# A two-layer trunk (attention with short convolution, gated linear attention, gated MLPs): GLA's state and read products are issued in one piece, the MLP's value weights are loaded before the gate's, and two small steps get a scheduling priority

## The chip, the cores and the metric

The kernel runs on one core of a Trainium2 chip. The core has a matrix engine (PE, TensorE), a vector engine (DVE, VectorE), a scalar engine (ACT, ScalarE), GpSimd (POOL) and a queue that issues DMAs (SP, SyncE). PE reads from SBUF and writes into PSUM, which has eight banks of 128 partitions by 512 float32 numbers; DVE and ACT read PSUM and SBUF and write SBUF. The metric is device time in microseconds (us) of one launch; the median over three runs of the kernel before is 1228.61 us (1227.54 to 1229.41).

## The reference

512 tokens, width 1024, two layers, all in float32. Cut to what matters here:

```python
def _sliding_window_sink_attention(q, k, v, sinks):      # layer 0, in blocks of 128 queries
    ...
    probs = jax.nn.softmax(jnp.concatenate([scores, sink], axis=-1), axis=-1)[..., :-1]
    out = jnp.einsum('bnhgqk,bnkhd->bnqhgd', probs.astype(v.dtype), vband)

def _gla_chunked(q, k, v, log_a):                        # layer 1: 4 heads, keys 128, values 256
    def step(state, inp):
        ...
        scores = jnp.einsum('bhtd,bhsd,bhtsd->bhts', qi, ki, decay)
        o_intra = jnp.einsum('bhts,bhsv->bhtv', scores, vi)
        state = jnp.exp(g_end)[..., None] * state + jnp.einsum(
            'bhsd,bhsv->bhdv', ki * jnp.exp(g_end[:, :, None, :] - gi), vi)
        return state, o_inter + o_intra                  # o_inter = (q * exp(g)) @ state

def _conv_ffn(h, w_up, conv_w, conv_b, w_down):          # each layer; w_up is 1024 x 5632
    u = _causal_depthwise_conv(h @ w_up, conv_w) + conv_b
    gate, up = jnp.split(u, 2, axis=-1)
    return (jax.nn.gelu(gate, approximate=False) * up) @ w_down
```

Each layer is a mixer (attention with a short convolution in layer 0, gated linear attention, GLA, in layer 1), then this MLP, then a per-layer embedding with a sigmoid gate.

## The kernel before

**Precision.** A float32 product is made of three fast passes. An operand is split into a high part (ACT copies it into the type fp32r) and a low part (DVE subtracts: source minus high part). `mm3` then issues high by high, high by low and low by high: L157, L158 and L159 for plain products, L848, L849 and L850 for the blocks of the seven-product scheme below. `cut` splits a piece of weights (high at L137, low at L138); `cut_blocks` does the same for blocks (high at L796, low at L797). Weights come by DMA on SP's queue into two buffers of 1 MB, `raw`; split parts live in three buffers each, `wh` and `wl`. Products go to PSUM banks of two rings of four, `ps` and `pa`. Small products (attention scores, GLA) run in full float32 with one instruction each in the code; the trace holds two records of each.

**Scheduling.** Except where an order is set by hand, a scheduler orders the instructions of each engine from the order in the program and from when their operands would be ready; `tc.high_priority(offset=n)` moves the instructions inside it up, as if they stood n earlier in the program. Semaphores between the engines follow from the tiles. A PSUM bank is tracked as a whole: a product into one half of a bank waits for a reader of the other half that stands earlier in the program.

**Attention (layer 0).** For each of four blocks of queries, `scores` (products L584) gives probabilities, `probs` transposes them (L631) and copies the transposed ones from PSUM to `pT`: ACT's copy at L638, and for the second half of the window DVE's at L636. The first block has only ACT's copies, two of them. `conv_taps` around it computes the short convolution; L682, L684 and L686 are its steps.

**Up-projection (`ffn`).** The 2816 columns of gate and of value are worked on in eleven groups of 256. For the gate's 256 columns, a block scheme with seven products in place of eight is used (`seven_forms`, `seven`): the piece `rg` is split as it is (`plain`), then DVE forms differences of blocks in place (L820, L821, L828, L830), which are split too: `t13`, `t2` (half as large, formed at L828 in `more_forms` and split at once in the program) and `last`. The value's 256 columns take plain products, in two halves: column block `w1` opens a group, `w0` comes in its middle. So each group has six splits, in the program's order w1, plain, t13, t2, w0, last. `loaded(d)` issues the two loads of group d, gate first, value second. The first of the two takes the buffer of the previous group's value piece, which is free after the low part of `w0`; the second takes that of the gate piece, free after the low part of `last`. PE's order in this stage is written by hand (`manual_schedule`): group d+1 opens with three quarters of the `w1` product, then steps of `seven` and parts of the value products alternate. ACT and DVE are ordered by the scheduler. Inside `seven`, ACT copies PSUM blocks from one bank to another between two products that add to them (L859, L860, L869, L873; L866 puts one aside). After a group, `taps` does the width-3 convolution (DVE L899, L902, L905, L908, ACT L906), ACT the Gelu (L1036), DVE the product of gate and value (L948 or L958).

**GLA (layer 1).** The list of calls at the end of the mixer sets the program's order; the scheduler fits the small products between projections. For head h, `base` forms cumulative decays and the product of even keys and queries (L1614); `diag` sums it over the partitions by a product with ones (L1620) and writes the diagonal of the score matrix `sc` (L1621, DVE); `decay` makes the decayed keys and queries of one level (DVE L1634 to L1642, ACT L1637); `level` multiplies them (L1655, for the coarsest level L1658) and writes them into `sc` (L1666, L1668); `level_pairs` does the two finest levels (L1693, L1699, L1704). `state` makes three products of decayed keys and values (L1750), two to a bank, and folds each into the running state `st` (first by ACT's copy L1757, then DVE's L1752). `read` makes for each of four chunks scores by values (L1773) and, but for the first, queries by state (L1775), two chunks to a bank, then squares and sums (ACT L1777). `turn` transposes (L1789) after a scaling by DVE (L1782).

Of the kernel before, what the change touches and what calls it, by code (L numbers as in the profile page):

```python
# [18 lines left out]
P = 128  # L19
# [37 lines left out]
class Kernel:  # L57
# [366 lines left out]
    def mixer0(self):  # L424
        nc, a, tc = self.nc, self.a, self.tc
        with tc.tile_pool(name="m0", bufs=1) as mp:
# [190 lines left out]
            def probs(t):  # L617

                s, den = ss[t], dens[t]
                w = 2 * P if t else P  # L620
                nc.vector.tensor_tensor(
                    s[:, 4:, :w], s[:, 4:, :w], den[:, 4:].unsqueeze(2).to_broadcast([P, 4, w]), ALU.mult
                )
                for head in range(4):
                    nc.scalar.activation(s[:, head, :w], s[:, head, :w], AF.Copy, scale=den[:, head : head + 1])
                pT = pTs[t] = mp.tile([P, 2, NQ, P], F32, tag="pT", name=self.nm("pT"), bufs=1)
                for g in range(2):
                    for c in range(2 if t else 1):
                        pb = self.pa()
                        for hh in range(4):  # L630
                            nc.tensor.transpose(  # L631
                                pb[:, hh * P : (hh + 1) * P], s[:, 4 * g + hh, c * P : (c + 1) * P], self.ident
                            )
                        o = pT[:, c, 4 * g : 4 * g + 4, :].rearrange("p a b -> p (a b)")
                        if c:
                            nc.vector.tensor_copy(o, pb)  # L636
                        else:
                            nc.scalar.copy(o, pb)  # L638

            def mix(t):  # L640

# [182 lines left out]
    def more_forms(self, ev, od):  # L824

        nc = self.nc
        b11, b21, b22 = ev[:, :, :P], od[:, :, :P], od[:, :, P:]
        nc.vector.tensor_tensor(b11, b22, b11, ALU.subtract)  # L828
        t2 = self.cut_blocks(b11, False)
        nc.vector.tensor_tensor(b21, b21, b11, ALU.subtract)  # L830
        return t2

# [46 lines left out]
    def ffn(self, i, project, next_gain):  # L879
# [8 lines left out]
        with tc.tile_pool(name=f"ffn{i}", bufs=1) as fp:  # L888
# [22 lines left out]
                    )  # L911

            def loaded(d):
                out = [self.raw(ND, 256) for _ in range(2)]
                for raw, c0 in zip(out, (256 * d, DFF + 256 * d)):
                    nc.sync.dma_start(raw, wu[:, :, c0 : c0 + 256])
                return out

# [6 lines left out]

            def prepare(d):

                rg, rv = loaded(d)
                w1 = column(rv, 1)
                ev, od = self.by_parity(rg)  # L930
                ws = self.seven_forms(ev, od, rg)
                return self.seven(od, ws, xg, self.forms), w1, column(rv, 0)
# [542 lines left out]
    def mixer1(self):  # L1475
# [4 lines left out]
        with tc.tile_pool(name="m1", bufs=1) as mp:  # L1480
# [261 lines left out]
            def state(h):  # L1742

                kt, tot = Fs[h, "kt"], Fs[h, "off"][2]
                st = mp.tile([P, NT - 1, GDV], F32, tag="st", name=self.nm("st"), bufs=1)
                for i in range(NT - 1):
                    if i % 2 == 0:
                        pp = self.pa()
                    u = pp[:, (i % 2) * GDV : (i % 2 + 1) * GDV]
                    mm(u, kt[:, i * P : (i + 1) * P], vt[i][:, h * GDV : (h + 1) * GDV], start=True, stop=True)  # L1750
                    if i:
                        nc.vector.scalar_tensor_tensor(  # L1752
                            out=st[:, i, :], in0=st[:, i - 1, :], scalar=tot[:, i, :], in1=u,
                            op0=ALU.mult, op1=ALU.add,
                        )
                    else:
                        nc.scalar.copy(st[:, i, :], u)  # L1757
                Fs[h, "st"] = st
# [3 lines left out]
            def read(h):  # L1762

                sc = scores[h]
                Ec, st = Fs[h, "off"][1], Fs[h, "st"]
                oss = self.few(NT, "ss")
                pos = []
                for j in range(NT):
                    if j % 2 == 0:
                        pp = self.pa()  # L1770
                    po = pp[:, (j % 2) * GDV : (j % 2 + 1) * GDV]
                    c = slice(j * P, (j + 1) * P)
                    mm(po, sc[:, c], vt[j][:, h * GDV : (h + 1) * GDV], start=True, stop=j == 0)  # L1773
                    if j:
                        mm(po, Ec[:, c], st[:, j - 1, :], start=False, stop=True)  # L1775
                    sq = self.sp.tile([P, GDV], F32, tag="sq", name=self.nm("osq"), bufs=2)
                    nc.scalar.activation(sq, po, AF.Square, accum_out=oss[:, j : j + 1])  # L1777
                    pos.append(po)
                rh = self.few(NT, "rq")
                self.rsqrt(rh, oss, 1.0 / GDV)  # L1780
                for j in range(NT):
                    nc.vector.tensor_scalar_mul(sc[:, j * GDV : (j + 1) * GDV], pos[j], rh[:, j : j + 1])  # L1782
# [33 lines left out]
            key(w, 1)  # L1816
            w = pair_w(256)
            base(0)
            decay(0, lo)
            query(w, 2)  # L1820
            diag(0)
            level(0, lo)
            decay(0, hi)
            decay_off(0)
# [114 lines left out]
```

## Time and profile before

| | us |
|---|---|
| median of three runs | 1228.61 (1227.54 to 1229.41) |
| the profiled execution's own time | 1228.92 |
| its span | 1227.1 |
| PE busy | 1217.1 |
| DVE busy | 970.1 |
| ACT busy | 665.0 |
| a 1 MB load of up-projection weights, from issue to landing (median of 44) | 5.0 |

The span is the time from the first to the last instruction of the profiled execution; its own time also holds what lies around the span. A row of a timeline gives the start from the span's start, the duration (for several instructions in a row, from the first's start to the last's end), the engine, the line of the kernel, the operation, the tile written and those read, the shape, the count, and in brackets how long the engine had been idle before it and what released it. Matmuls are pipelined: each is listed with a duration longer than the step from one to the next.

### The profile page before, as it was taken

What the parts mean: (1) busy time and instruction counts of PE and PEld (TensorE: products, weight loads), DVE (VectorE), ACT (ScalarE), POOL (GpSimd) and SP (SyncE); (2) the same over time, 40 slices, a digit from 0 to 9 for tenths busy, and PEclk for the clock granted to TensorE, in tenths of its full rate; (3) what the DMA queues carried; (4) which work ended last, traced back from release to release, by engine and by line L of the source; (5) the groups of instructions that cost most, each with busy time, mean ns of one, the idle gap of its engine ahead of it and who ended that gap; (6) DMA issues with size and microseconds to landing.
All of it is one profiled execution on the core that took longest, in us unless ns stands there. A gap on an engine that the chain in (4) does not pass through costs nothing.

```text
span 1227.1 us, 17714 instructions
## 1 busy us (share of the span) xinstructions
PE 1217.1 (99%) x7028; PEld 1053.4 (86%) x7028; DVE 970.1 (79%) x1537; ACT 665.0 (54%) x1084; POOL 44.2 (4%) x64
## 2 busy tenths in 40 slices
PE   9999999999999999999999999999999999999998
PEld 8877789989999889888978978889998989889887
DVE  6886587899998986746679875777999889987595
ACT  7466455556555644534563644555555545645374
POOL 3500000000000000000100000000000000000000
PEclk9999999999999999999999999999999999999999
DMA  7221322423232332222332212323242422422601
GB/s 217 92 82 51 90 69 69 138 69 127 80 109 98 100 124 95 95 93 87 113 91 69 85 53 69 103 66 107 69 138 69 138 69 96 144 96 95 205 1 69
DMA packets 111128, 117.61 MB, mean 96 GB/s; under 512 B 2841, under 2 KB 106323, under 8 KB 111045
## 3 DMA queue, kind: packets, MB, share of 16 engines
q1 hardware_dynamic: 109680, 115.35, 28.9%
q8 instruction: 55, 0.90, 0.3%
q0 software_dynamic: 560, 0.42, 0.3%
q10 hardware_dynamic: 804, 0.70, 0.2%
q14 instruction: 29, 0.23, 0.1%
HBM read 114.37 MB, written 2.10 MB: 95 GB/s over the span
## 4 chain that ended last, share of the span: by engine, by line
PE 83%; DVE 10%; ACT 2%; issue 2%; DMA 2%; POOL 1%; DVEq 0%; ACTq 0%; POOLq 0%
PE ps L157 13%; PE ps L158 12%; PE ps L159 12%; PE pa L158 6%; PE pa L157 6%; PE pa L159 6%; PE ps L850 5%; PE ps L848 5%; PE ps L849 5%; PE pa L850 2%; PE pa L849 2%; PE pa L848 2%; DMA raw<-in_ffn_w_up_dram 2%; DVE wl L138 1%; DVE wl L797 1%
## 5 line engine op out<-in xcount | busy, mean ns | idle before, releaser
L137 ACT ACTIVATE wh<-raw 128x1024 fp32r<-128x1024 f32 (+4 forms) x154 | 152.2, 991 | 162.2 <-PE ps L158 112.8
L138 DVE TENSOR_TENSOR wl<-raw,wh 128x1024 fp32r<-128x1024 f32 (+4 forms) x154 | 175.2, 1139 | 50.5 <-ACT wh L137 48.9
L796 ACT ACTIVATE wh<-raw 128x1024 fp32r<-128x1024 f32 x78 | 82.4, 1056 | 113.7 <-DVE raw L821 66.6
L908 DVE SCALAR_TENSOR_TENSOR zt<-z,vfa,zt 128x510 f32<-128x510 f32 (+1 forms) x176 | 131.4, 747 | 9.6 <-ACT zt L906 8.8
L797 DVE TENSOR_TENSOR wl<-raw,wh 128x1024 fp32r<-128x1024 f32 x78 | 95.4, 1223 | 14.5 <-ACT wh L796 14.4
L906 ACT ACTIVATE zt<-z,vfb 128x512 f32<-128x512 f32 x88 | 70.6, 808 | 17.0 <-DVE four L958 5.4
L157 PE MATMUL ps<-b,wh 128*128 128x512 f32 x192 | 76.8, 400 | 0.0
L159 PE MATMUL ps<-b,wl 128*128 128x512 f32 x192 | 75.7, 394 | 0.0
L158 PE MATMUL ps<-b,wh 128*128 128x512 f32 x192 | 75.4, 393 | 0.0
L159 PE MATMUL pa<-b,wl 128*128 128x512 f32 x176 | 68.7, 390 | 0.4 <-DVE wl L138 0.4
L157 PE MATMUL pa<-b,wh 128*128 128x512 f32 x176 | 69.0, 392 | 0.0
L157 PE MATMUL pa<-a,wh 128*128 128x512 f32 x176 | 69.0, 392 | 0.0
L158 PE MATMUL pa<-b,wh 128*128 128x512 f32 x176 | 69.0, 392 | 0.0
L158 PE MATMUL pa<-a,wh 128*128 128x512 f32 x176 | 69.0, 392 | 0.0
L159 PE MATMUL pa<-a,wl 128*128 128x512 f32 x176 | 68.6, 390 | 0.0
L850 PE MATMUL ps<-four,wl 128*128 128x256 f32 x232 | 65.7, 283 | 0.0
L849 PE MATMUL ps<-four,wh 128*128 128x256 f32 x232 | 65.6, 283 | 0.0
L848 PE MATMUL ps<-four,wh 128*128 128x256 f32 x232 | 65.6, 283 | 0.0
L157 PE MATMUL ps<-a,wh 128*128 128x512 f32 x160 | 63.1, 394 | 0.0
L158 PE MATMUL ps<-a,wh 128*128 128x512 f32 x160 | 62.5, 391 | 0.0
L159 PE MATMUL ps<-a,wl 128*128 128x512 f32 x160 | 62.4, 390 | 0.0
L157 PE MATMUL ps<-uh,wh 128*128 128x512 f32 x128 | 50.3, 393 | 0.0
(470 smaller groups left out, 3526.8 us busy)
## 6 DMA issues: line engine op xcount, KB each, us to landing
raw<-in_ffn_w_up_dram SPq DMA_DIRECT2D x44, 1024.0 KB, 5.0
raw<-in_ffn_w_down_dram SPq DMA_DIRECT2D x13, 1024.0 KB, 4.8
raw<-in_hy_w_in_dram SPq DMA_DIRECT2D x8, 1024.0 KB, 5.0
raw<-in_gla_w_in_dram SPq DMA_DIRECT2D x8, 1024.0 KB, 5.1
raw<-in_ffn_w_down_dram SPq DMA_DIRECT2D x8, 768.0 KB, 4.2
raw<-in_ple_w_gate_dram SPq DMA_DIRECT2D x6, 1024.0 KB, 4.8
raw<-in_hy_w_out_dram SPq DMA_DIRECT2D x16, 256.0 KB, 3.9
raw<-in_gla_w_out_dram SPq DMA_DIRECT2D x4, 1024.0 KB, 4.7
```

What stands on the lines that cost most here:

```text
L137: nc.scalar.activation(hv, v, AF.Copy)
L138: nc.vector.tensor_tensor(lv, v, hv.bitcast(F32), ALU.subtract)
L157: mm(out, lh, rh, start=start, stop=False, **kw)
L158: mm(out, lh, rl, start=False, stop=False, **kw)
L159: mm(out, ll, rh, start=False, stop=stop, **kw)
L796: nc.scalar.activation(h, src, AF.Copy)
L797: nc.vector.tensor_tensor(l, src, h.bitcast(F32), ALU.subtract)
L848: mm(out, wh, xh, start=first and j == 0, stop=False, **kw)
L849: mm(out, wh, xl, start=False, stop=False, **kw)
L850: mm(out, wl, xh, start=False, stop=j == ND // 2 - 1, **kw)
L906: nc.scalar.activation(y, z, AF.Identity, scale=w2[:, f : f + 1], bias=bb[:, f : f + 1])
L908: nc.vector.scalar_tensor_tensor(out=y[:, tap:], in0=z[:, : S - tap], scalar=w[:, f : f + 1], in1=y[:, tap:], op0=ALU.mult, op1=ALU.add,)
```

## The change

Six edits in the program's text:

- `probs`: the copies of the first block's probabilities get a priority of 100 positions; those of the other blocks one of 0.
- `more_forms`: the split of `t2`, high and low part, gets a priority of 40.
- `loaded` and `prepare`: the value's piece is allocated and loaded first, the gate's second. The splits stay in the same order.
- `state`: all three products are issued first, then the three steps that read them.
- `read`: all products of the four chunks are issued first, then the four squares.
- the list of calls: `diag(0)` stands ahead of `decay(0, lo)` and `query(w, 2)` instead of behind them.

```diff
                         o = pT[:, c, 4 * g : 4 * g + 4, :].rearrange("p a b -> p (a b)")
-                        if c:
-                            nc.vector.tensor_copy(o, pb)
-                        else:
-                            nc.scalar.copy(o, pb)
+                        with tc.high_priority(offset=0 if t else 100):
+                            if c:
+                                nc.vector.tensor_copy(o, pb)
+                            else:
+                                nc.scalar.copy(o, pb)
...
         nc.vector.tensor_tensor(b11, b22, b11, ALU.subtract)
-        t2 = self.cut_blocks(b11, False)
+        with self.tc.high_priority(offset=40):
+            t2 = self.cut_blocks(b11, False)
         nc.vector.tensor_tensor(b21, b21, b11, ALU.subtract)
...
                 out = [self.raw(ND, 256) for _ in range(2)]
-                for raw, c0 in zip(out, (256 * d, DFF + 256 * d)):
+                for raw, c0 in zip(out, (DFF + 256 * d, 256 * d)):
                     nc.sync.dma_start(raw, wu[:, :, c0 : c0 + 256])
...
-                rg, rv = loaded(d)
+                rv, rg = loaded(d)
...
+                us = []
                 for i in range(NT - 1):
                     if i % 2 == 0:
                         pp = self.pa()
-                    u = pp[:, (i % 2) * GDV : (i % 2 + 1) * GDV]
-                    mm(u, kt[:, i * P : (i + 1) * P], vt[i][:, h * GDV : (h + 1) * GDV], start=True, stop=True)
+                    us.append(pp[:, (i % 2) * GDV : (i % 2 + 1) * GDV])
+                    mm(us[i], kt[:, i * P : (i + 1) * P], vt[i][:, h * GDV : (h + 1) * GDV], start=True, stop=True)
+                for i, u in enumerate(us):
                     if i:
...
                         mm(po, Ec[:, c], st[:, j - 1, :], start=False, stop=True)
+                    pos.append(po)
+                for j, po in enumerate(pos):
                     sq = self.sp.tile([P, GDV], F32, tag="sq", name=self.nm("osq"), bufs=2)
                     nc.scalar.activation(sq, po, AF.Square, accum_out=oss[:, j : j + 1])
-                    pos.append(po)
...
             base(0)
+            diag(0)
             decay(0, lo)
             query(w, 2)
-            diag(0)
             level(0, lo)
```

In the order of instructions that results on each engine, PE's order changes in GLA alone: `diag(0)`'s product stands 24 matmuls earlier, and the products of `state` and `read` stand together where a projection matmul stood between them before. In the up-projection the orders of ACT and DVE change, and on SP which of a group's two pieces is loaded first. No instruction is added or removed.

## The prediction

> **What bounds the kernel now.** I read the page's head first, then the table of windows over three stages, then PE's own waits, then the timelines around each wait.
>
> ```profile
> PE 1217.1 (99%) x7028; PEld 1053.4 (86%) x7028; DVE 970.1 (79%) x1537; ACT 665.0 (54%) x1084; POOL 44.2 (4%) x64
> ```
>
> TensorE (PE) is busy for 99% of the span. So nothing that only shortens VectorE (DVE) or ScalarE (ACT) pays; what pays is PE time lost to a late operand. The change adds and removes no product, so it can win only such lost time. The windows cover the two up-projections (from the first value product of the first group to that of the tenth) and one crowded piece of GLA; the columns are the stretch's length, then busy time of PE, weight load, DVE, ACT, POOL, the granted clock and the DMA share.
>
> ```profile
> 205.12:395.83 190.71, 190.20 (x1191) 171.73 (x1189) 172.72 (x231) 109.06 (x155) 0.00 (x0) 1.00 0.30 100
> 837.21:1028.45 191.24, 190.35 (x1191) 171.76 (x1190) 171.28 (x230) 108.18 (x154) 0.00 (x0) 1.00 0.30 100
> 640.00:660.00 20.00, 18.85 (x126) 15.27 (x124) 19.62 (x47) 7.18 (x14) 0.00 (x0) 1.00 0.12 36
> ```
>
> The granted clock is 1.00 throughout, so time is counted in products and stalls alone. PE's waits (line that waited, what released it, total, times, longest):
>
> ```profile
> PE pa L1655 <- DVE sc L1621: 1.1, 1, 1.1
> PE ps L850 <- DVE t L797: 1.0, 2, 0.5
> PE pa L584 <- ACT pT L638: 1.0, 1, 1.0
> PE pa L159 <- DVE wl L138: 0.4, 1, 0.4
> PE pa L158 <- DVE wl L138: 0.2, 1, 0.2
> PE pa L1658 <- DVE sc L1621: 0.2, 1, 0.2
> ```
>
> These six lines sum to 3.9 us, and they are all in places that the change touches. The list understates: ends of matmuls are modelled, so the loss is better read from start to start. In the up-projection the first window starts with its first group; the next group starts at 226.16, so that one that runs without a visible wait takes 226.16 - 205.12 = 21.04 us:
>
> ```profile
> 226.16 0.40 PE L157 MATMUL pa<-a,wh 128*128 128x512 f32 x1
> ```
>
> Nine such groups are 189.36 us. The two windows above last 190.71 and 191.24, so 1.35 and 1.88 us are lost in them, 3.2 together, where the waits list shows only 1.6. The Trainium skill ("Perfetto Trace Analysis", the note that opens the page) calls matmul busy time a bad metric because matmuls are pipelined; the 3.2 against 1.6 agrees. A sum made from the waits list alone would be 1228.9 - 3.9 = 1225.0.
>
> **Up-projection: values loaded first, t2's split ahead.** Each group needs two 1 MB pieces, gate and value. Today the gate's goes out first, when the value's last split has freed a buffer, and the value's second, when the gate's last split has. But the next group starts with a value product. The activity on the raw pieces around the second group, and ACT and DVE there:
>
> ```profile
> L916 SPq DMA_DIRECT2D raw<-in_ffn_w_up_dram x2: 368/368/368, 214.7 to 217.8; - x2
> ```
> ```profile
> 223.97 1.06 ACT L137 ACTIVATE wh<-raw 128x1024 fp32r<-128x1024 f32 x1 [1.62 <-DMA raw<-in_ffn_w_up_dram]
> ```
> ```profile
> 225.06 1.23 DVE L138 TENSOR_TENSOR wl<-raw,wh 128x1024 fp32r<-128x1024 f32 x1 [0.89 <-ACT wh L137]
> ```
>
> The gate goes out at 214.7, the value at 217.8; it lands 6.2 us later, ACT makes the high part (1.06), DVE the low part, done at 226.29, while the group starts at 226.16. That is a loop load, split, load with no reserve, and its jitter is the 0.4 and 0.2 of L159 and L158 and the smaller slips that only the windows show. After the change the value takes the issue at 214.7: landing 220.9, high part 222.0, low part by 223.2, 3 us before its use. The gate goes out at 217.8 and lands at 224.0; its first low part is done by 224.0 + 1.06 + 1.23 = 226.3, and PE reaches the first gate product after three quarters of the value product, eighteen matmuls of 0.23 (723.57 to 723.80 in the last fence of this part): 4.2 us into the group, at 230.4. Reserve 4 us. Both places in SyncE's (SP's) queue stay taken by the same size, in exchanged order; no other load is passed. As w1's split no longer ends the loop, the group's splits all move up, until PE itself is what frees their buffers.
>
> t2's low part (0.69 us on DVE) stands, in the changed order, straight behind L830, the form after t2's own; today w0's 1.23 us split slips in between:
>
> ```profile
> 255.61 0.69 DVE L830 TENSOR_TENSOR raw<-raw 128x512 f32<-128x512 f32 x1
> 256.21 1.23 DVE L138 TENSOR_TENSOR wl<-raw,wh 128x1024 fp32r<-128x1024 f32 x1
> 257.34 0.69 DVE L797 TENSOR_TENSOR t<-raw,t 128x512 fp32r<-128x512 f32 x1
> ```
> ```profile
> 257.31 0.28 PE L849 MATMUL ps<-four,t 128*128 128x256 f32 x1
> 258.09 0.39 PE L850 MATMUL ps<-four,t 128*128 128x256 f32 x1 [0.50 <-DVE t L797]
> ```
>
> PE steps from L849 to L850 in 0.78 instead of 0.12, a loss of 0.66; with t2 first its low part would run from 256.21 to 256.9, before L850's 257.43; its high part is there, since PE's first two products of t2 had begun. w0's split then ends 0.6 later, near 258.0, and its low part is used after the ten steps of 0.12 that t2's twelve still have, and two of 0.23: 257.43 + 1.2 + 0.46 = 259.1. The second such stall (the waits list counts two) goes the same way. I take 3.0 of the 3.2 us. Bounds: 1.4 (the t2 stalls and the L159 one, 0.5 + 0.5 + 0.4 by the waits list) and 3.2.
>
> **Copies of the probabilities (first block).** ACT copies two halves; the second has to wait behind a convolution step that itself waits for DVE:
>
> ```profile
> 72.19 0.57 ACT L638 COPY pT<-pa 128x512 f32<-128x512 f32 x1
> 73.25 0.72 ACT L684 ACTIVATE cy<-pad,vec 128x512 f32<-128x512 f32 x1 [0.48 <-DVE pad L682]
> 73.88 0.57 ACT L638 COPY pT<-pa 128x512 f32<-128x512 f32 x1
> ```
>
> With the priority the second copy stands straight behind the first: start 72.66 instead of 73.88, 1.22 us sooner. PE's L584 waited for exactly this copy (1.0 by the list). L684 moves back by 0.57; behind it on ACT and DVE stand the steps of the convolution, whose result no product in this stretch reads, and were that cover gone, the 0.57 would come back. I take 1.2; bounds 1.0 and 1.4, since PE cannot start before its previous group of L584 is out.
>
> **GLA: diag(0) earlier.** In the second half of head 0 PE's scores (L1655) wait for a PSUM bank that the diagonal's scaling (L1621) has to leave, the 1.1 of the list. DVE there:
>
> ```profile
> 639.71 0.43 DVE L1641 TENSOR_TENSOR F<-F,kT 128x256 f32<-128x256 f32 x1
> 640.04 0.70 DVE L1523 SCALAR_TENSOR_TENSOR qT<-ps,R 128x512 f32<-128x512 f32 x1
> 640.64 0.43 DVE L1621 TENSOR_TENSOR sc<-pa,cf 128x256 f32<-128x256 f32 x1
> ```
>
> The diagonal's product needs only one product of keys and queries (L1614), which this row ends at 632.62:
>
> ```profile
> 632.22 0.40 DVE L1614 TENSOR_TENSOR F<-kT,qT 128x256 f32<-128x256 f32 x1
> ```
>
> Issued ahead of decay and query, it runs on PE near 632.6 and L1621 follows on DVE about 635. PE's next bound at L1655 is then the operand of L1641, ready at 640.14, minus the 0.43 that L1621 no longer takes there: about 639.7, against 641.07 now. PE reaches L1655 1.1 before it starts there, near 640.0. So the wait goes but for a rest. Against it: PE may wait 0.2 at 632.6 for L1614, and DVE is busy 19.62 of 20 us here, so what is put earlier pushes other DVE work back by 0.43. I take 0.9; bounds 0.5 and 1.3.
>
> **GLA: state and read products in one piece.** Two products share one PSUM bank; today the first one's reader stands between them, so PE runs a projection matmul in the gap. Head 0's state:
>
> ```profile
> 679.87 1.03 PE L1750 MATMUL pa<-vt,F 128*128 128x256 f32 x4
> 680.54 0.50 PE L157 MATMUL ps<-wh,b 128*128 128x336 f32 x1
> 680.92 0.70 PE L1750 MATMUL pa<-vt,F 128*128 128x256 f32 x2
> 681.27 0.50 PE L158 MATMUL ps<-wl,b 128*128 128x336 f32 x1
> 681.61 0.32 PE L159 MATMUL ps<-wh,b 128*128 128x336 f32 x1
> 681.77 0.32 PE L157 MATMUL ps<-wh,b 128*128 128x336 f32 x1
> ```
>
> From 680.54 to 681.61 run two projection matmuls at 0.16 each (681.61 to 681.77) and one product at 0.335 (two in 679.87 to 680.54): 0.655 of work in 1.07, 0.41 lost to the wait and to changing over twice. Issued together, PE changes over once. In the order of the changed kernel eight such pieces close up: four of state, four of reads. The cheapest that I found is in head 2's state:
>
> ```profile
> 723.57 0.39 PE L159 MATMUL ps<-b,wl 128*128 128x512 f32 x1
> 723.80 0.59 PE L1750 MATMUL pa<-vt,F 128*128 128x256 f32 x2
> 724.04 0.59 PE L157 MATMUL ps<-b,wh 128*128 128x512 f32 x1
> 724.46 0.40 PE L158 MATMUL ps<-b,wh 128*128 128x512 f32 x1
> ```
>
> 0.89 for two matmuls of 0.23 and one product: 0.1 lost. Eight pieces are worth 0.8 to 3.3; I take 1.2, near the low end, because most of them stand among such 512-wide matmuls, and because for two heads PE waits shortly after for DVE (L1658, 0.2), which swallows what is won before it. If that takes all, the term is 0. The readers now start one product later. The Trainium skill ("Perfetto Trace Analysis", Matmuls) says that independent groups of matmuls should rotate through PSUM banks so that one's evacuation overlaps the next one's matmuls; the change does the opposite inside a bank. In the row above PE had other banks' work to go on with, so I let the rule cost nothing. If all eight delays of 0.335 reached PE, the term would be 1.2 - 2.7 = -1.5 and the time 1225.2.
>
> **Sum.** 3.0 + 1.2 + 0.9 + 1.2 = 6.3 us.
>
> ```profile
> span 1227.1 us, 17714 instructions
> ```
>
> The profiled execution took 1228.92 us (span 1227.1 and 1.8 around it), 0.3 above the median of 1228.61, so the changed kernel's own time is 1222.6 by the one and 1222.3 by the other: 1222.5. With all lower bounds (1.4, 1.0, 0.5, 0) the gain is 2.9, 1225.9; with all upper ones (3.2, 1.4, 1.3, 3.3) it is 9.2, 1219.6.
>
> **Rivals.** (1) *Slower: the gate's Gelu now stands ahead of a PSUM copy.* In the order of the changed kernel ACT's Gelu, which waits for DVE's last convolution tap (L908), comes ahead of the copy L869 in nine of the twenty groups that have one. PE needs that copy at its next gate product. The seventh group today:
>
> ```profile
> 344.32 0.36 ACT L869 COPY ps<-ps 128x256 f32<-128x256 f32 x1
> 346.83 1.06 ACT L1036 ACTIVATE zt<-zt 128x1024 f32<-128x1024 f32 x1 [2.15 <-DVE zt L908]
> ```
> ```profile
> 346.54 0.28 PE L848 MATMUL ps<-four,wh 128*128 128x256 f32 x1
> ```
>
> If the Gelu still began at 346.83, the copy would end at 346.83 + 1.06 + 0.36 = 348.25, and PE would stand for 1.7 us, nine times: 15.4 us, 1237.9. It decides at 346.54 - 1.42 = 345.12: the taps must end 1.7 us sooner than now. For it: DVE is busy 172.7 of 190.7 us in this stage. Against it: w1's split (1.23) leaves the stretch before the taps for an idle one (0.89 of wait ahead of L138 above), and w0's and the gate's last split stand behind the taps in the new order. Half-way, at 0.85 each, it is 7.7 us and eats the gain: 1230.2.
>
> (2) *The loads change places, and the stall goes with them.* The gate's 1 MB is late instead of the value's. Then only t2's two stalls (1.3 by 0.66 each) go, of the 3.0: 1222.5 + 1.7 = 1224.2; if those stay too, since DVE is as full as before, 1225.5. For it: the loop keeps its length, and only its late end changes hands. Against it stands the 4 us reserve.
>
> (3) *GLA gives nothing.* DVE is full there, and both GLA terms (2.1) turn into later waits: 1224.6. If instead each of the eight readers is waited for one product longer (the rule on banks above, 0.335 each), it is the 1225.2 worked out there.
>
> (4) *Nothing to be had.* Another operand is nearly as late at each place, the gain stays below 2.5 us: about 1227.5.
>
> **How the numbers follow.** My forecast 0.52, (1) 0.13, (2) 0.13, (3) 0.12, (4) 0.10. This measurement can tell about 0.2% (2.5 us) from no change, so faster means below 1226.1 and slower above 1231.1. Faster: 0.52 + 0.12 + 0.11 of (2) = 0.75. Slower: 0.10 of (1). Same: the rest, 0.15. The likeliest case alone spans 1219.6 to 1225.9; the range goes up to 1229 to take in (4) and leaves most of (1) out.
>
> **What would show it.** In the changed profile: L584's wait, L1655's wait and both waits of L850 for t are gone from PE's list; two value products 21.04 us apart in every group; the load ahead of each group's first split lands more than 2 us before it; in GLA the L1750 records come in runs of six with no L157 among them, and L1658's wait for DVE is the line that grows. Wrong would be a wait of PE for ACT's copy at L869's place (rival 1), one for the gate's first low part (rival 2), or a new wait in GLA of about a microsecond (rival 3).

## The result, and the profile after

| | before | after |
|---|---|---|
| median | 1228.07 us (6 runs, 1227.22 to 1229.41) | 1222.99 us (6 runs, 1222.46 to 1223.74) |
| ratio after to before | | 0.9958, 95% interval 0.9945 to 0.9970 |
| span of the profiled execution | 1227.1 us | 1221.4 us |
| DVE busy | 970.1 us | 972.5 us |

5.1 us faster by the medians, 5.7 by the spans. The forecast was 1222.5, made from a median before of 1228.61 over three runs. The head of the page of the changed kernel, and what its PE waited for (line that waited, what released it, total, times, longest):

```profile
span 1221.4 us, 17724 instructions
## 1 busy us (share of the span) xinstructions
PE 1213.9 (99%) x7028; PEld 1054.8 (86%) x7028; DVE 972.5 (80%) x1537; ACT 663.1 (54%) x1084; POOL 43.6 (4%) x64
```

```profile
PE pa L192 <- DVE mhalf L181: 1.3, 1, 1.3
PE pa L1661 <- DVE sc L1707: 0.5, 1, 0.5
PE pa L631 <- ACT pT L639: 0.4, 1, 0.4
PE ps L157 <- DVE kT L1532: 0.3, 1, 0.3
PE pa L1661 <- DVE sc L1624: 0.2, 1, 0.2
PE pa L158 <- DVE wl L138: 0.2, 1, 0.2
```

The line numbers of the changed kernel are one to six higher: L639 is the old L638, L1661 the old L1658, L1707 the old L1704, L1532 the old L1529. The old waits for pT at L584, for the diagonal at L1655 and for t at L850 are gone. Three that were not on the list stand in their place: L631 for a copy of pT, a projection's L157 for a key's bank, and L1661 for L1707. The list alone would make the gain 2.3 us (5.2 less 2.9, the start's 1.3 in both), less than half of it. So the account is made from start to start: since both kernels issue the same number of matmuls (7028 records), the start of each record after can be compared with that of the record of the same number before. The difference at a boundary, less that at the boundary before it, is what a stage gave (us; the boundaries are times of the kernel before, at places where both have the same matmul):

| stage | forecast | after |
|---|---|---|
| start, to 60 | 0 | +0.82 |
| attention, 60 to 205 | -1.2 | -0.38 (-1.19 at 74, then +0.81) |
| first up-projection, 205 to 396 | -1.3 | -1.36 |
| down-projection and on, 396 to 631 | 0 | -0.25 |
| diag(0), 631 to 642 | -0.9 | -1.05 |
| 642 to 670 | 0 | +0.61 |
| state and read, 670 to 760 | -1.2 | -1.95 |
| second up-projection, 837 to 1028 | -1.7 | -1.88 |
| rest | 0 | -0.22 |
| sum | -6.3 | -5.66 |

The forecast named 3.0 for the two up-projections together; it is split here as their windows split 3.2. The 0.25 comes near the 608th us, in a stage without an edit; that stage lies between -0.27 and +0.16 in the runs below, so this is taken as chance. Of the last 0.22, 0.21 is a loss that the kernel before had in the tenth group of its second up-projection, just behind the window of nine. These are the same two windows in the changed kernel, with the columns as before:

```profile
205.55:394.91 189.36, 189.36 (x1190) 171.70 (x1189) 174.53 (x233) 108.55 (x155) 0.00 (x0) 1.00 0.31 101
833.64:1023.00 189.36, 189.36 (x1190) 171.71 (x1189) 173.73 (x231) 108.41 (x155) 0.00 (x0) 1.00 0.31 101
```

Both are nine times 21.04 us to the hundredth, PE is busy in every one of them, and no lost PE time is left there. Around the second group in the changed kernel (the loads; ACT's high part and DVE's low part of w1; PE's first product of the group):

```profile
L919 SPq DMA_DIRECT2D raw<-in_ffn_w_up_dram x2: 368/368/368, 214.9 to 217.9; - x2
DMA to landing us min/median/max: 6.3/6.3/6.3
```
```profile
222.47 1.05 ACT L137 ACTIVATE wh<-raw 128x1024 fp32r<-128x1024 f32 x1
223.55 1.23 DVE L138 TENSOR_TENSOR wl<-raw,wh 128x1024 fp32r<-128x1024 f32 x1
226.59 0.40 PE L157 MATMUL pa<-a,wh 128*128 128x512 f32 x1
```

The value lands near 221.2 and the high part starts 1.3 us later, no longer waiting for the load; the low part is done at 224.78, 1.8 us before the group.

### The profile page after: what moved, and what is told of

Read it like the earlier page. It is cut to its first block, busy times and chain, and to the rows that moved or that the text cites. A ratio compares the mean times of both kernels' runs of the same rounds, so it can differ in the third digit from the quotient of the medians.

```text
span 1221.4 us, 17724 instructions
## 1 busy us (share of the span) xinstructions
PE 1213.9 (99%) x7028; PEld 1054.8 (86%) x7028; DVE 972.5 (80%) x1537; ACT 663.1 (54%) x1084; POOL 43.6 (4%) x64
## 4 chain that ended last, share of the span: by engine, by line
PE 87%; DVE 8%; ACT 2%; issue 2%; POOL 1%; DVEq 0%; ACTq 0%; POOLq 0%
PE ps L157 12%; PE ps L158 12%; PE ps L159 12%; PE pa L158 7%; PE pa L157 7%; PE pa L159 7%; PE ps L850 6%; PE ps L852 6%; PE ps L851 6%; PE pa L852 2%; PE pa L851 2%; PE pa L850 2%; DVE wl L138 1%; PE ps L1349 1%; PE ps L1348 1%
## 5 line engine op out<-in xcount | busy, mean ns | idle before, releaser
L157 PE MATMUL ps<-b,wh 128*128 128x512 f32 x192 | 76.6, 399 | 0.0
L158 PE MATMUL ps<-b,wh 128*128 128x512 f32 x192 | 74.9, 390 | 0.0
L157 PE MATMUL pa<-b,wh 128*128 128x512 f32 x176 | 69.1, 392 | 0.0
L157 PE MATMUL pa<-a,wh 128*128 128x512 f32 x176 | 69.1, 392 | 0.0
L158 PE MATMUL pa<-b,wh 128*128 128x512 f32 x176 | 69.0, 392 | 0.0
L158 PE MATMUL pa<-a,wh 128*128 128x512 f32 x176 | 69.0, 392 | 0.0
L850 PE MATMUL ps<-four,wh 128*128 128x256 f32 x232 | 65.6, 283 | 0.0
L157 PE MATMUL ps<-a,wh 128*128 128x512 f32 x160 | 63.1, 394 | 0.0
L158 PE MATMUL ps<-a,wh 128*128 128x512 f32 x160 | 62.6, 391 | 0.0
L157 PE MATMUL ps<-uh,wh 128*128 128x512 f32 x128 | 50.3, 393 | 0.0
```

What stands on the lines that cost most here:

```text
L157: mm(out, lh, rh, start=start, stop=False, **kw)
L158: mm(out, lh, rl, start=False, stop=False, **kw)
L850: mm(out, wh, xh, start=first and j == 0, stop=False, **kw)
```

## The experiments

Each kernel was built on the kernel before or on the changed one. Times come from 5 to 11 runs beside runs of the kernel before on the same chip. Most of these effects are no larger than the interval of a ratio, so the verdicts rest on the starts of the same matmuls, read as above from one profile each. The intervals of e2, e3 and e4 contain 1: by time alone these three can't be told from no change.

| run | median, us | ratio (95% interval) | start | attention | up 1 | diag | 642-670 | state, read | up 2 |
|---|---|---|---|---|---|---|---|---|---|
| after | 1222.99 | 0.9958 (0.9945-0.9970) | +0.82 | -0.38 | -1.36 | -1.05 | +0.61 | -1.95 | -1.88 |
| e1_loads | 1225.91 | 0.9981 (0.9972-0.9990) | +0.24 | +0.08 | -1.35 | 0 | 0 | 0 | -1.88 |
| e2_t2 | 1228.31 | 1.0002 (0.9993-1.0011) | +0.24 | +0.05 | -0.50 | 0 | 0 | 0 | -0.85 |
| e3_probs | 1228.07 | 0.9997 (0.9988-1.0005) | +0.78 | -0.37 | -0.56 | 0 | 0 | 0 | -1.25 |
| e4_diag0 | 1227.88 | 0.9996 (0.9987-1.0005) | +0.64 | +0.03 | -0.71 | -1.03 | +0.62 | 0 | -0.07 |
| e5_oneblock | 1226.80 | 0.9987 (0.9978-0.9996) | +0.48 | +0.05 | +0.14 | 0 | 0 | -1.94 | +0.44 |
| e6_not2 | 1223.74 | 0.9960 (0.9946-0.9973) | +1.05 | -0.37 | -1.35 | -1.06 | +0.61 | -1.95 | -1.88 |
| f2_soft | 1222.96 | 0.9957 (0.9944-0.9969) | +0.63 | -0.54 | -1.36 | -1.06 | +0.60 | -1.95 | -1.88 |
| f3_diags | 1225.30 | 0.9976 (0.9966-0.9985) | 0 | -0.37 | -1.35 | -1.03 | +0.62 | +0.14 | -1.88 |
| g2_pairs_soft | 1224.53 | 0.9967 (0.9955-0.9980) | +0.68 | -0.50 | -1.36 | -1.04 | +0.56 | -0.66 | -1.88 |
| h1_actcopy | 1222.96 | 0.9955 (0.9942-0.9969) | +0.85 | -0.50 | -1.35 | -1.05 | +0.24 | -1.94 | -1.88 |

(0 stands for less than 0.06.) The two up-projection columns of e3, e4 and e5 are the key to one of the errors: these three kernels leave the up-projection as it was, and yet it differs. Group by group, part of the loss is the same in every profile with the old order of loads: the fifth group takes 21.3 us and the eighth at least 21.2 in place of 21.04, and the third at least 21.2 in all of them, some 1.2 us over both stages. The rest comes and goes: the third group of the first stage took 21.25 or 22.0 (21.5 in e2_t2), the eighth of the second 21.2 or 22.4.

**e1_loads: the loads alone.** On the kernel before:

```diff
-                for raw, c0 in zip(out, (256 * d, DFF + 256 * d)):
+                for raw, c0 in zip(out, (DFF + 256 * d, 256 * d)):
...
-                rg, rv = loaded(d)
+                rv, rg = loaded(d)
```

> The kernel before with one part of the change alone: value piece loaded first, gate second. Theory A (the up-projection's losses, 1.35 us in the first and 1.88 us in the second by the windows of the kernel before, all hang on the loop load, split, load; once the value comes first all splits of a group move up, t2's too): both stages fall to nine times 21.04 = 189.4 us, t2's two stalls (0.66 each, start to start) are gone with the value's, and the whole is 3.2 us faster, ratio 0.9974. Theory B (t2's stall is a matter of DVE's order alone, w0's split standing ahead of t2's): the two t2 stalls stay, about 1.3 us, and the gain is 1.9 us, ratio 0.9985. The rest of the trace, from the start to the first up-projection and GLA, keeps its steps under both.

Measured: both up-projections lose nothing any more (-1.35 and -1.88, all that the windows had shown), and PE has no wait for t:

```profile
PE pa L192 <- DVE mhalf L181: 1.3, 1, 1.3
PE pa L1655 <- DVE sc L1621: 1.2, 1, 1.2
PE pa L584 <- ACT pT L638: 1.0, 1, 1.0
PE pa L158 <- DVE wl L138: 0.2, 1, 0.2
PE pa L1658 <- DVE sc L1621: 0.2, 1, 0.2
```

(e1_loads, PE's waits; the wait of L158 lies in the first 20 us, here and in the kernels before and after.) Theory A holds: the loads carry the whole effect. By time it is 2.6 us (1228.48 to 1225.91), less than theory A's 3.2, though its ratio of 0.9974 lies inside the interval.

**e2_t2: t2's priority alone.** On the kernel before:

```diff
-        t2 = self.cut_blocks(b11, False)
+        with self.tc.high_priority(offset=40):
+            t2 = self.cut_blocks(b11, False)
```

> The kernel before with t2's split alone given the priority. Theory B (the parts add up): the two stalls of 0.66 us at t2 go, and nothing else in the up-projection, gain 1.3 us (ratio 0.9989); the waits for w1's low part (0.4 and 0.2 in the waits list) stay. Theory A (the loop of loads is what makes DVE late): the stall at t2 goes too, but since the last load of each group still closes the loop, the loss shows again at the next group's first value product, so that the gain is under 0.7 us.

Measured: ratio 1.0002. A wait for t of 0.2 is left, and the wait for w1's low part is longer (0.7 against 0.4, one execution each), as theory A has it (e2_t2, PE's waits):

```profile
PE pa L159 <- DVE wl L138: 0.7, 2, 0.5
PE ps L157 <- ACT vt L1509: 0.2, 1, 0.2
PE ps L851 <- DVE t L797: 0.2, 1, 0.2
```

The stages show -0.50 and -0.85, but kernels with an unchanged up-projection differ by as much, and the tenth group of the second one, behind the window, lost 0.82 (0.21 in the kernel before). What t2's priority is worth alone can't be told from nothing here.

**e6_not2: the changed kernel without t2's priority.**

```diff
-        with self.tc.high_priority(offset=40):
-            t2 = self.cut_blocks(b11, False)
+        t2 = self.cut_blocks(b11, False)
```

> The changed kernel without the priority of t2's split. Theory A (with the value loaded first all splits have moved up and t2's priority has nothing left to win): both up-projections stay at nine times 21.04 = 189.4 us without a wait for t, and the time is the changed kernel's, ratio 0.9958 within 0.0005. Theory B (t2's place in DVE's order counts by itself): waits of PE for t of up to 0.66 us come back, two or more of them, ratio 0.9968 or above.

Measured: both up-projections as in the changed kernel within a hundredth, no wait for t, ratio 0.9960. Theory A holds: beside the loads, this edit does nothing that can be measured. (The two profiled executions differ by 1.3 us, 1224.55 against 1223.25: 0.2 at the start, 0.3 between the 396th and the 631st us, and 0.8 in the last stage, none of it in the up-projection. The runs of the two kernels overlap.)

**e3_probs: the copies of the probabilities alone.** On the kernel before:

```diff
-                        if c:
-                            nc.vector.tensor_copy(o, pb)
-                        else:
-                            nc.scalar.copy(o, pb)
+                        with tc.high_priority(offset=0 if t else 100):
+                            if c:
+                                nc.vector.tensor_copy(o, pb)
+                            else:
+                                nc.scalar.copy(o, pb)
```

> The kernel before with the probabilities' copies alone given the priority. From the trace of the changed kernel: PE gains 1.19 us at the 74th us, and of it 0.81 us is given back before the 140th, at the transposition of the second block and after it. Theory A (given back to the softmax of the next block on DVE: the convolution's steps now stand among its maxima, and the chain had only some 0.5 us to spare): net gain at the first up-projection 0.4 us, whatever the start of the run does, with a new wait of about 0.4 us of PE for a copy of pT near the 89th us. Theory B (the give-back is only the late start of that one execution, 0.8 us lost in the first 10 us, which the softmax had kept): with a start like the kernel before's, the gain stays 1.2 us and the new wait isn't there.

Measured: -1.19 at the 74th us, then +0.65 by the 90th and +0.17 by the 140th, net -0.37, and the wait of L631 for pT (0.4) is there. Its start was late by 0.78 as well, so this run alone does not decide; f3_diags, whose start is the kernel before's to the hundredth, does: also -1.19, +0.65, +0.17. Theory A holds. DVE has no gap there of more than 0.04 us, before and after. These are two steps of the convolution (L686, in the changed kernel L687) and the end of the eighth and last of the maxima of the next block's scores (L593), in the kernel before and in the changed one:

```profile
74.27 0.75 DVE L686 SCALAR_TENSOR_TENSOR cy<-pad,vec,cy 128x512 f32<-128x512 f32 x1
75.27 0.75 DVE L686 SCALAR_TENSOR_TENSOR cy<-pad,vec,cy 128x512 f32<-128x512 f32 x1
78.34 0.09 DVE L593 DVE_READ_ACCUMULATOR2_ANT mx<- 128x1 f32 x1
```
```profile
75.42 0.75 DVE L687 SCALAR_TENSOR_TENSOR cy<-pad,vec,cy 128x512 f32<-128x512 f32 x1
76.43 0.75 DVE L687 SCALAR_TENSOR_TENSOR cy<-pad,vec,cy 128x512 f32<-128x512 f32 x1
79.16 0.09 DVE L593 DVE_READ_ACCUMULATOR2_ANT mx<- 128x1 f32 x1
```

The first maximum is at 74.93 before and at 75.08 after, so that one convolution step stands among the maxima before and two do after; DVE has the same work to do up to the last maximum either way. PE comes to the scores 1.2 us sooner, but the last maximum ends at 79.25, against 78.43 before: 0.82 later, which is this run's late start and nothing else. So the softmax did not move at all, and PE ran into it: DVE set its time already in the kernel before.

**f2_soft: the maxima first.** On the changed kernel, in `scores`:

```diff
-                            nc.vector.tensor_tensor_reduce(
...
+                            with tc.high_priority(offset=60 if t == 1 else 0):
+                                nc.vector.tensor_tensor_reduce(
```

> The changed kernel with the maxima of the second block's scores (DVE, eight of them) also given a priority, of 60, which puts one of the two convolution steps that stood among them behind three more of them. Theory A (the gain of the copies is given back because DVE is full between the 72nd and the 79th us of the changed kernel, with the convolution's 0.75 us steps among the maxima): the maxima end 0.7 us sooner unless the other step still holds them, PE's wait of 0.4 us for a copy of pT near the 90th us goes, and 0.4 to 0.6 us more stay won than in the changed kernel, ratio near 0.9954. Theory B (the give-back comes from the copies themselves or from ACT): no change in the steps from the 74th to the 140th us.

Measured: give-back 0.66 in place of 0.81, the wait 0.3 in place of 0.4, ratio 0.9957. The reason for the small yield is on DVE (f2_soft, the end of the maxima; here L594 is the maxima, L688 the convolution, L601 what follows the maxima):

```profile
78.29 0.09 DVE L594 DVE_READ_ACCUMULATOR2_ANT mx<- 128x1 f32 x1
78.29 0.75 DVE L688 SCALAR_TENSOR_TENSOR cy<-pad,vec,cy 128x512 f32<-128x512 f32 x1
78.96 0.16 DVE L601 SCALAR_TENSOR_TENSOR nm<-mx,sink 128x8 f32<-128x8 f32 x1
```

The maxima end 0.68 sooner (78.38 less a start of 0.63, against 79.25 less 0.82), but the second convolution step now stands between them and L601, which starts only 0.13 sooner. That is about the 0.15 won. Theory A has the mechanism, not the size: it expected 0.4 to 0.6 and the wait gone.

**e4_diag0: diag(0) alone.** On the kernel before:

```diff
             base(0)
+            diag(0)
             decay(0, lo)
             query(w, 2)
-            diag(0)
```

> The kernel before with diag(0) alone moved ahead. Theory A (what it wins stays but for a rest): PE's wait of 1.1 us at the finer scores of head 0 goes, 1.05 us between the projection matmuls around it, and of it 0.5 us comes back at a later projection's first matmul that waits for DVE to free its bank (L1532 in the trace of the changed kernel, near the 662nd us), so net 0.5 us. Theory B (that later wait comes from the state and read products, not from diag(0)): net 1.05 us, and no wait for a key's bank near the 662nd us.

Measured: -1.03, then +0.62 with the new wait for a key's bank, net -0.41. Theory A. In the changed kernel this is the place, on DVE and on PE:

```profile
660.49 1.22 DVE L1611 TENSOR_TENSOR_SCAN G<-run,la 128x512 f32<-128x512 f32 x1
661.74 0.69 DVE L1532 TENSOR_TENSOR kT<-ps,R 128x512 f32<-128x512 f32 x1
```

```profile
662.49 0.42 PE L157 MATMUL ps<-wh,b 128*128 128x336 f32 x1 [0.34 <-DVE kT L1532]
```

The fourth bank that the next projection needs still holds the key, and DVE, with no gap of more than 0.04 us since the 640th us, comes to it only after a 1.22 us scan. DVE does not come to the key any sooner for the edit: the key's step starts at 662.87 in the kernel before and at 662.65 in e4_diag0, where PE had entered this stage 0.30 earlier. PE alone is ahead, and meets it.

**h1_actcopy: one copy less on DVE.** On f2_soft:

```diff
-                        nc.vector.tensor_copy(second(A[:b], b), second(pl[:b], b))
+                        nc.scalar.copy(second(A[:b], b), second(pl[:b], b))
```

> The kernel of the run f2_soft with the copy of the coarsest scores out of PSUM (0.41 us each, one for every head) on ACT in place of DVE. Theory A (the wait of PE for a key's bank near the 662nd us, which ate half of diag(0)'s gain, is DVE being full from the 640th us on): a copy less on DVE there brings the key's step 0.3 to 0.4 us forward, the wait of 0.3 us (0.51 start to start) is nearly gone, and the coarsest scores' two waits lose up to 0.4 us too; ratio 0.9952. Theory B (the wait is the scan's place ahead of the key's step, which stays): the step of 0.5 us in the trace there stays, time as f2_soft's within 0.3 us.

Measured: the step is +0.24 in place of +0.60, and the wait is gone from the list. This shows that DVE being full makes the wait; the order of scan and key stayed as it was. Putting the key ahead of the scan, which might take away the rest, was not tried. The waits at the coarsest scores did not shrink. In time it is 1222.96, the same as the changed kernel's 1222.99: a third of a microsecond in the trace is too little to be seen.

**e5_oneblock: state and read alone.** On the kernel before:

```diff
-                    u = pp[:, (i % 2) * GDV : (i % 2 + 1) * GDV]
-                    mm(u, kt[:, i * P : (i + 1) * P], vt[i][:, h * GDV : (h + 1) * GDV], start=True, stop=True)
+                    us.append(pp[:, (i % 2) * GDV : (i % 2 + 1) * GDV])
+                    mm(us[i], kt[:, i * P : (i + 1) * P], vt[i][:, h * GDV : (h + 1) * GDV], start=True, stop=True)
+                for i, u in enumerate(us):
...
+                    pos.append(po)
+                for j, po in enumerate(pos):
...
-                    pos.append(po)
```

> The kernel before with state's and read's products alone issued in one piece. In the trace of the changed kernel the stretch of these products (from the 670th to the 760th us of the kernel before) is 1.95 us shorter. Theory A (the pieces do it alone): 1.9 us less in that stretch, with two new waits of PE of together 0.7 us for DVE at the coarsest scores of heads 2 and 3, and ratio 0.9984. Theory B (they need diag(0)'s earlier place, without which DVE is later and those two waits grow): under 1.2 us in the stretch. Nothing else changes by more than chance; the later projection's wait for a key's bank near the 662nd us is absent under both, since that is diag(0)'s.

Measured: -1.94 in the stretch, with L1658's two waits (0.5 and 0.2). They are not new: the step from the matmul ahead into head 2's first L1658 was 0.45 us before and is 0.87, head 3's was 0.75 and is 0.63. Theory A: the two edits in GLA add up. In the changed kernel head 0's state reads:

```profile
678.26 1.46 PE L1754 MATMUL pa<-vt,F 128*128 128x256 f32 x6
679.37 0.50 PE L157 MATMUL ps<-wh,b 128*128 128x336 f32 x1
679.71 0.32 PE L158 MATMUL ps<-wl,b 128*128 128x336 f32 x1
```

Six records in a row from 678.26 to 679.37, 0.37 a product, and one change of 0.19 to the projection (0.34 from L157 to L158 in place of 0.15), where two stood before.

Not all of the 1.94 was won in the pieces themselves. The eight transposes of head 1's `turn` (L1789) take 1.63 us in the kernel before, with two steps of 0.39 among them in place of 0.11. They read what DVE's scaling (L1782) writes. DVE's scaling and PE's transposes, in the kernel before and in e5_oneblock (three lines higher there):

```profile
717.18 1.66 DVE L1782 TENSOR_SCALAR sc<-pa,rq 128x256 f32<-128x256 f32 x4 [0.90 <-POOL rq L167]
717.87 1.79 PE L1789 MATMUL pa<-cf,sc 128*128 128x128 f32 x8
```
```profile
716.86 1.66 DVE L1785 TENSOR_SCALAR sc<-pa,rq 128x256 f32<-128x256 f32 x4 [0.90 <-POOL rq L167]
718.48 1.03 PE L1792 MATMUL pa<-cf,sc 128*128 128x128 f32 x8
```

The scaling now starts 1.62 us ahead of the transposes, in place of 0.69. It hangs, by way of GpSimd's L167, on the last square of the read, and the read's products now end sooner. The transposes take 0.87 us from start to the next product in all seven kernels with this edit and 1.61 to 1.64 in the five without it. So 0.76 us came from a wait of another step, which PE's list of waits does not show.

**f3_diags: diag(2) and diag(3) moved too.** On the changed kernel:

```diff
             base(2)
+            diag(2)
...
-            diag(2)
...
             base(3)
+            diag(3)
...
-            diag(3)
```

> The changed kernel with diag(2) and diag(3) moved ahead too, each right behind its base as diag(0) now is. Theory A (the two waits that the state products now run into, of 0.71 and 0.40 us start to start, are for a bank that the diagonal or the pairs leave late, as in head 0): both go, some 0.8 us less between the 670th and the 725th us, ratio near 0.9951. Theory B (the bank is left late because DVE as a whole is behind there): the waits move to the coarsest scores and to the reads, which stand earlier now, and the stretch is not shorter, or longer by up to 1 us.

Measured: the stretch is 2.1 us longer than in the changed kernel (+0.14 against -1.95), worse than theory B allowed. One wait does most of it:

```profile
PE pa L1623 <- DVE F L1617: 1.4, 1, 1.4
```

L1623 is the diagonal's product, here of head 2, and L1617 the one product on DVE that it needs (the old L1614). For head 0 the earlier place asked 0.2 of PE; for a later head PE is stopped for 1.4, with all its matmuls behind it, because DVE has not formed the operand.

**g2_pairs_soft: the finest levels' copies first.** On f2_soft, in `level_pairs`:

```diff
-                for u in (0, 64):
+                with tc.high_priority(offset=120):
+                  for u in (0, 64):
```

> The kernel of the run f2_soft with a priority of 120 for the copies of the two finest levels (DVE L1702, L1707 in the changed kernel's lines), which puts the second pair of them ahead of the decay's steps; PE's coarsest scores (L1661) of heads 2 and 3 move up to stand right behind the state products. Theory A (L1661 waits for a bank only because those copies stand behind other DVE work): the two waits of together 1.1 us start to start shrink to under 0.5, some 0.5 us less between the 670th and the 725th us, ratio 0.9953. Theory B (PE arrives as much sooner as DVE does): the waits stay as they are or grow, and the time is that of f2_soft, 0.9957 within 0.0005.

Measured: 1.3 us worse than f2_soft (-0.66 against -1.95); PE's L1661 moved up further than DVE did. It is theory B's mechanism, but worse than it allowed: both waits for L1707 (here L1709) are now 0.56 long.

```profile
PE pa L1662 <- DVE sc L1709: 1.1, 2, 0.6
```

## Why the prediction was right, and where it was off

The time, 1222.99 against 1222.5, is right, with two terms too large and one too small. The gain is less close: 6.3 us were forecast, 5.1 came by the medians, partly because the median before came out at 1228.07 over six runs. In the profile the stages with an edit gave 6.0.

- **Bound.** "It can win only such lost time" held: all the gains of more than a quarter of a microsecond lie in the stages where the waits were. "They are all in places that the change touches" was wrong of one line: L158's 0.2 lies in the first 20 us, so the up-projection's part of the list is 1.4. Counting from start to start, as forecast, is what brought the size near. By the waits list alone it would have been 1225.0.
- **Up-projection, 3.0.** The mechanism is shown by e1_loads and e6_not2, in a stronger form than forecast: the loads are the whole of it, t2's priority has no measurable part. The piece that lands is w1's, as worked out (DVE's first low part starts at 223.55 and the group at 226.59); the low part is done 1.8 us ahead of the group, in place of the 3 forecast, since ACT was still at the Gelu and a copy. The sign "more than 2 us" between landing and first split came in only four of the 17 groups whose landing the trace has; in the others it is 0.6 to 1.9 us. In the kernel before it was at most 0.05 us in 14 of 16: there the first split stood waiting for the load. The size was taken from one execution. In four profiles with the old order of loads and splits (before, e3, e4, e5) the two stages lost 3.2, 1.4, 2.4 and 3.8 us, 2.7 on average, and e1_loads won 2.6 in time. "Nine such groups are 189.36 us" was exact. Some 1.2 us above it were lost in every one of these executions; how much more is lost differs between them, and the forecast read one of them as the loss. What decides it was not looked into.
- **Copies of the probabilities, 1.2.** The step that failed is that the gain stays: "behind it on ACT and DVE stand the steps of the convolution, whose result no product in this stretch reads". True, but those steps share DVE with the maxima of the next scores, which were not looked at, and DVE had no gap before them. The 1.2 came (1.19) and 0.8 went again; net 0.4.
- **diag(0), 0.9.** Won 1.05, of which 0.6 came back 20 us later, net 0.4. "What is put earlier pushes other DVE work back" named the cause; the price was not followed to the key's bank. h1_actcopy shows that DVE's load has a part in it: with 0.41 us less on DVE, 0.24 came back in place of 0.60.
- **State and read, 1.2.** It was 1.95, inside the bounds. The sum had no term for head 1's transposes, which gave 0.76 of it by waiting no longer for DVE's scaling; without them it is 1.2, as forecast. The caution taken for L1658's wait was right in kind: the two steps into it took 1.20 us together before and 1.50 after, which is already in the 1.95.
- **Rivals.** (1) did not come. The Gelu stands ahead of the copy in ten of the twenty groups, not in nine, but in the seventh group it began at 343.09 and the copy behind it ended at 344.42, 1.4 us before PE's need at 345.78. The taps did end sooner by more than was asked. (2) did not come; the gate's piece is not late anywhere. (3) came in part: of 3.0 won in GLA, 0.6 went again. The rule on rotating banks that the Trainium skill has ("Perfetto Trace Analysis", Matmuls) cost nothing that shows here: PE's list in e5_oneblock has no wait for a state or read product's own bank.

That the sum was so close is partly luck: too much by 0.8 in the copies, by 0.3 to 0.4 in the loads (against the average of profiles and against e1_loads) and by 0.5 in diag(0), too little by 0.75 in state and read, where a wait went that nobody had counted.

## What to carry to other kernels

Where an operand's load is chained to the end of the work on the one before, look at which of several loads the next stage reads first, and give it the buffer that is free first; here a priority inside the stage then had nothing left to win. A wait that is taken away is worth what the next engine in the chain can follow: before counting it whole, look for the next time the fast engine meets the busy one, and read that engine's gaps (none above 0.04 us here, twice). The same may work the other way: where products end sooner, a wait further down the chain can go too, as at head 1's transposes. A small product may be moved ahead only as far as its operand on the other engine has been: in f3_diags a product that came too early held PE for 1.4 us, with everything behind it.

## What the runs showed of the hardware

The same code at the start takes up to 0.8 us more in some executions. The first eight transposes (L462, from 4.4 us on) step by 0.21 us and then, from some moment on, by 0.11. In the kernel before and in f3_diags all of them step by 0.11; in e1_loads and e2_t2 only the first two steps are of 0.21; in the changed kernel and in h1_actcopy all are. PE's timeline of the kernel before and of the changed one:

```profile
4.42 0.60 PE L462 MATMUL ps<-cf,xin 128*128 128x128 f32 x4
```
```profile
4.47 1.05 PE L462 MATMUL ps<-cf,xin 128*128 128x128 f32 x4
```

The granted clock is shown as 1.00 in both. The Trainium skill ("TensorE: Matmul & The Clock Gate", "Wait — 56ns, not 53.3ns?") has 106.7 ns for 128 columns before the array has warmed up and 55.6 ns after; an estimate with two passes for each transpose gives 0.213 and 0.111. The two steps agree with it, though the trace lists one record for each transpose and so does not show the passes. The 512-column matmuls of L192 around them show the same change, from steps of 0.43 to steps of 0.23 us. What decides the moment was not tried. Together with what hangs on it, the start lies between 0 and 1.05 us later than the kernel before's profile in the eleven others, a wider spread than the 0.4 us net that the copies' edit or diag(0)'s brought, so that spans alone could not have shown these two.
